# A conformer convolution beside a DeltaNet scan: when GpSimd joins in, where the channel sums stand, which PSUM banks the copies take

## The chip, the cores and the metric

The kernel runs on one core of one Trainium2 chip. A core has five engines that work side by side, each through a queue of its own in order: TensorE (PE, matmuls, with its weight loads shown apart as PEld), VectorE (DVE), ScalarE (ACT), GpSimd (POOL) and SyncE (SP, which here only starts transfers). The metric is the device time of one execution in microseconds, as a median of repeated executions.

## The reference, cut to what matters

One layer on 512 frames of 2048 channels, in float32. A shared projection `proj = h @ w_in` feeds two mixers. Branch A is a gated DeltaNet: 16 heads, a short convolution, a recurrence over chunks of 64 frames, and `y_a = o_a @ w_br_a`. Branch B is a convolution module. What the change touches:

```python
u = jax.nn.glu(glu_in, axis=-1)                 # 16 blocks of 128 channels x 512 frames
u = causal_depthwise_conv(u, w_dw[i]) + b_dw[i] # 31 taps
u = jax.nn.silu(layernorm(u, ln_g[i], ln_b[i])) * jax.nn.silu(z_b)
y_b = u @ w_br_b[i]
mixed = (gate_a * y_a + gate_b * y_b) @ w_out[i]
x = x + rmsnorm(mixed, g_post[i])
e = p[i] @ w_ple_proj[i]
x = x + rmsnorm(jax.nn.sigmoid(x @ w_ple_gate[i]) * e, g_ple[i])
```

The layer norm runs over the channels, so it needs the sum of all 16 convolved blocks.

## The kernel before, in words

**Products.** A float32 product is made of three matmuls on rounded halves: high by high, high by low, low by high (L184, L186, L188 for a block of `proj`; L1090, L1092, L1094 for the branches; L1548 to L1550 for the last product). Weights come in pieces of 128 x 512. For each, SP loads `raw`, ACT casts the high half (L127) and L128 subtracts to get the low half `w`; four pieces fit in the ring, and the program prepares each up to three pieces ahead of its use. `low_part[0]` names the engine that does L128: DVE at first, GpSimd from a certain place in the program, DVE again from the layer norm on. In the stage of branch A a piece serves 12 matmuls of 512 columns.

**Stages.** About 50 to 510 us: gate products. 530 to 1494: `q`, `k`, `v` blocks for the heads, with the recurrence of each group of heads (`group`, `head_scan`) woven in between. 1494 to 1845: the rest of the GLU blocks and branch A. 1846 to 1925: layer norm. To 2094: branch B. To 2260: `w_out` by a Strassen scheme, with the steps of the post norm (`post`) at its end, first for the lower 256 frames (LOW) and then for the upper (HIGH). To 2436: the last product, `gemm_tm`. The rest is the tail.

**Weaving.** Side work is written as generators. `tick()` follows each matmul; a generator moves on when as many matmuls have passed as it yielded. A scheduler then sets each engine's queue from the order of the program; `pin` keeps an instruction in the order in which it was written. Whatever stands in an engine's queue waits for what stands ahead of it.

**The convolution.** `evac_glu_b` (sigmoid on ACT) and `evac_glu_a` (product on DVE, L981) leave a block `sg` in SBUF. `convs` takes the blocks that wait, one after another: `near` starts `y` on ACT (L933) and 30 taps on DVE follow (L954), the accumulator `uc` in SBUF. The first channel begins while the recurrence still runs, with `sg` read from SBUF. Once the PSUM pool `ups` exists, `near` first copies the block to PSUM (L930, `up`), and the taps read `up`. `side_convs` does two of the 16 channels on ACT (products, L972) and GpSimd (sums, L973). `filtered` gathers the channel sum `acc` on GpSimd: a copy for the first channel (L918), an addition for the others (L920).

**At the end of the recurrence** stand, for each pair of heads, L733 (DVE), L735 (GpSimd), L739 (DVE, the normed output `O`), L744 (PE, transposes `po`) and L749 (DVE, out of `po`). After it the pools of the heads close: two PSUM banks of weight sums and four of the scan come free. Four of `yps` and two of `ups` are taken in their place. `split_oa` makes the halves of the heads' outputs (L1067 on ACT, L1069 on GpSimd).

**Later steps.** `branch` sums a block of y over 16 pieces into four banks and evacuates them (L1102). `layer_norm` sums over channels with a matmul by ones (`sum_ps`, L1143), and later spreads the reciprocal deviation with another (`rstd_ps`, L1170). `post` scales, adds x again (L1460), transposes (L1466) and splits (L1470).

Of the kernel before, what the change touches and what calls it, by code (L numbers as in the profile page):

```python
# [12 lines left out]
ALU = mybir.AluOpType  # L13
# [4 lines left out]
NTT = T // P  # L18
D = 2048
NK = D // P  # L20
# [7 lines left out]
CP = 10  # L28
# [53 lines left out]
def _body(ctx, tc, A, out):  # L82
    nc = tc.nc
    PSUM = bass.MemoryType.PSUM
# [209 lines left out]
    def stepper(gen, n=1):  # L294
        def f(k=None):
            for _ in range(n):
                next(gen, None)
        return f
# [605 lines left out]
    waiting = deque()  # L904
    taken = set()
    scanning = [-1]

    def evac_glu_b(i):
        def f(ps):
# [5 lines left out]
    def filtered(i, y):  # L915
        if not acc:
            acc.append(slots.tile([P, T], F32, tag="s", name="acc"))
            nc.gpsimd.tensor_copy(acc[0], y)  # L918
        else:
            nc.gpsimd.tensor_tensor(acc[0], acc[0], y, ALU.add)  # L920
        done.add(i)

    def near(held=True):
# [10 lines left out]
        return i, u, y  # L934

    def pace(s):
        return (3 + s % 2) if ups else CP

    def convs():
        ready = last = None  # L940
        while scanning[0] < NH // 2 - 1:
            yield 4
        while len(done) < NK:
            ready = ready or near()
            if not ready:
                if last and len(taken) == NK:
                    filtered(*last)
                    last = None
                yield 1
                continue  # L950
            (i, u, y), ready = ready, None
            w0 = V_DW + i * TAPS
            for s in range(1, TAPS):
                pin(nc.vector.scalar_tensor_tensor(y[:, s:], u[:, 0:T - s], vv(w0 + TAPS - 1 - s), y[:, s:], ALU.mult, ALU.add))  # L954
                if s == 28 and last:
                    filtered(*last)
                    last = None
                if s == 24:
                    ready = near()
                yield pace(s)  # L960
            nc.sync.dma_start(u_dram[i], y)
            last = i, y

    def side_convs():
        for _ in range(SIDE):
            while not waiting:
                yield 1
            i, u, y = near(False)
            w0 = V_DW + i * TAPS
            for s in range(1, TAPS):  # L970
                pr = s2.tile([P, T], F32, tag="s2", name="pr")
                nc.scalar.activation(pr[:, s:], u[:, 0:T - s], AF.Copy, scale=vv(w0 + TAPS - 1 - s))  # L972
                pin(nc.gpsimd.tensor_tensor(y[:, s:], y[:, s:], pr[:, s:], ALU.add))  # L973
                yield 18
            nc.sync.dma_start(u_dram[i], y)
            filtered(i, y)
# [75 lines left out]
    s2_ctx = ExitStack()  # L1052
    lop = s2_ctx.enter_context(tc.tile_pool(name="lop", bufs=LOP))
    s2 = s2_ctx.enter_context(tc.tile_pool(name="s2", bufs=40 - LOP))
    yps = s2_ctx.enter_context(tc.tile_pool(name="yps", bufs=4, space=PSUM))
    ups = s2_ctx.enter_context(tc.tile_pool(name="ups", bufs=2, space=PSUM))
    cpool[:] = [s2, "s2"]
    low_part[0] = nc.gpsimd

    def low(n, name, dt=F32R):  # L1060
        return lop.tile([P, T], dt, tag="lop", name=name) if n < LOP else s2.tile([P, T], dt, tag="s2", name=name)
# [14 lines left out]
    def branch(W, j, q, lhs, evac, side=None):  # L1076
        prep_src.extend([W[j, 2 * q], W[j, 2 * q + 1]])

        def job():
            if q == 0:  # L1080
                branch_ps[j] = [yps.tile([P, T], F32, tag="y", name="yp") for _ in range(NTT)]
            ps = branch_ps[j]
            for k in range(4 * q, 4 * q + 4):
                wh, wl = next_piece()
                if side:
                    side(k)
                for tt in range(NTT):
                    b = slice(tt * P, (tt + 1) * P)
                    lh, ll = lhs[k]
                    mm(ps[tt], lh[:, b], wh, start=k == 0, stop=False)  # L1090
                    tick()
                    mm(ps[tt], lh[:, b], wl, start=False, stop=False)  # L1092
                    tick()
                    mm(ps[tt], ll[:, b], wh, start=False, stop=k == NK - 1)  # L1094
                    tick()
            if q == 3:
                for tt in range(NTT):
                    evac(j, tt, ps[tt])
        jobs.append(job)

    def evac_ya(j, tt, ps):
# [32 lines left out]
    def layer_norm():  # L1134
        for i in range(NK):
            while i not in done:
                yield
            u_t[i] = hp("ur")
            nc.sync.dma_start(u_t[i], u_dram[i])
            yield 1  # L1140
        low_part[0] = nc.vector
        pm = ups.tile([P, T], F32, tag="u", name="sum_ps")
        mm(pm, ones, acc[0], start=True, stop=True)  # L1143
        mean = ups.tile([P, T], F32, tag="u", name="mean_ps")
        nc.scalar.activation(mean, pm, AF.Copy, scale=1.0 / D)
        acc2 = hp("acc2")
        yield 6
        for i in range(NK):
            u = u_t[i]
            pin(nc.vector.tensor_tensor(u, u, mean, ALU.subtract))  # L1150
            sq = hp("lsq") if i else acc2
            nc.scalar.activation(sq, u, AF.Square)
            if i:
                pin(nc.vector.tensor_tensor(acc2, acc2, sq, ALU.add))
            yield 7
        pvr = ups.tile([P, T], F32, tag="u", name="var_ps")
        for tt in range(NTT):
            mm(pvr[:, tt:tt + 1], acc2[:, tt * P:(tt + 1) * P], ones[:, 0:1], start=True, stop=True)
        var = lnp.tile([P, NTT], F32, name="var")
        nc.vector.tensor_scalar(var, pvr[:, 0:NTT], 1.0 / D, EPS, ALU.mult, ALU.add)  # L1160
        rst = lnp.tile([P, NTT], F32, name="rst")
        nc.gpsimd.tensor_tensor(rst, var, mhalf_c[:, 0:NTT], ALU.pow)
        dg = hp("dg")
        for tt in range(NTT):
            nc.vector.tensor_scalar(dg[:, tt * P:(tt + 1) * P], ident, rst[:, tt:tt + 1], None, ALU.mult)
        for i in range(3):
            load_zb(i)
        yield 12
        rstd = ups.tile([P, T], F32, tag="u", name="rstd_ps")
        mm(rstd, ones, dg, start=True, stop=True)  # L1170
        yield 6
        for i in range(NK):
            u = u_t[i]
            pin(nc.vector.tensor_tensor(u, u, rstd, ALU.mult))
            nc.scalar.activation(u, u, AF.Silu, scale=vv(V_LNG + i), bias=vv(V_LNB + i))
            yield 6
            if i + 3 < NK:
                load_zb(i + 3)
            nc.vector.tensor_tensor(u, u, zb[i], ALU.mult)
            uh = low(0, "uh")  # L1180
            nc.scalar.copy(uh, u)
            ul = low(LOP if i < 33 - LOP else 0, "ul")
            nc.vector.tensor_tensor(ul, u, uh.bitcast(F32), ALU.subtract)
            uT[i] = (uh, ul)
            yield 6
# [269 lines left out]

    def post(tts, xr):
        rm = inv_rms(ssm[:, tts[0]:tts[0] + 2, :], f"m{tts[0]}")
        for j in range(4):
            for n, tt in enumerate(tts):
                nc.vector.scalar_tensor_tensor(x1[tt][j], x1[tt][j], rm[:, n:n + 1], xr.pop((tt, j)), ALU.mult, ALU.add)  # L1460
            yield
            for k2 in (2 * j, 2 * j + 1):
                ps = bank()
                for n in range(4):
                    k = 2 * k2 + n // 2
                    nc.tensor.transpose(ps[:, n * P:(n + 1) * P], x1[tts[n % 2]][j][:, (k % 4) * P:(k % 4 + 1) * P], ident)  # L1466
                xh = unit(HP_, "xh", F32R)
                nc.scalar.copy(xh, ps)
                xl = unit(HP_, "xl", F32R)
                nc.vector.tensor_tensor(xl, ps, xh.bitcast(F32), ALU.subtract)  # L1470
                x1T[k2, tts[0] // 2] = (xh, xl)
                yield
# [67 lines left out]
    def gemm_tm(lhs, evac, tts=ALL, side=None):  # L1540
        ps = {tt: bank() for tt in tts}
        for k in range(NK):
            wh, wl = next_piece()
            if side:
                side(k)
            for tt in tts:
                lh, ll = lhs(k, tt)
                mm(ps[tt], lh, wh, start=k == 0, stop=False)  # L1548
                mm(ps[tt], lh, wl, start=False, stop=False)  # L1549
                mm(ps[tt], ll, wh, start=False, stop=k == NK - 1)  # L1550
        for tt in tts:
            evac(tt, ps[tt])
# [52 lines left out]
    gp = bcast_row(A["g_ple"], 0)  # L1605
    load_e(0)
    pgen = post(HIGH, xr)
    gemm_tm(x1_lhs, ple_evac(0, gp), LOW, stepper(pgen))
    for _ in pgen:
        pass  # L1610
    gemm_tm(x1_lhs, ple_evac(0, gp), HIGH)
# [87 lines left out]
```

## Time and profile before

| | |
|---|---|
| median of 3 runs | 2446.0 us (2445.83 to 2446.65) |
| the profiled execution | 2447.55 us, span 2445.8 us |
| mean granted TensorE clock | 0.998 |
| PE busy | 2414.0 us (99%) |
| DVE busy | 1792.4 us (73%) |
| ACT busy | 1208.8 us (49%) |
| POOL busy | 507.0 us (21%) |

Times in the views count from the start of the span. In a row of the timeline stand the start, the busy time, the engine, the line and operation, what is written from what, and in brackets the engine's idle time just before it and what ended that. A row of waits names the engine and its line, what released it, and then the total, the number and the longest. A row of windows has, for each engine, the busy time and in brackets the instructions, then the granted clock, the share of the transfers and GB/s.

### The profile page before, as it was taken

What the parts mean: (1) busy time and instruction counts of PE and PEld (TensorE: products, weight loads), DVE (VectorE), ACT (ScalarE), POOL (GpSimd) and SP (SyncE); (2) the same over time, 40 slices, a digit from 0 to 9 for tenths busy, and PEclk for the clock granted to TensorE, in tenths of its full rate; (3) what the DMA queues carried; (4) which work ended last, traced back from release to release, by engine and by line L of the source; (5) the groups of instructions that cost most, each with busy time, mean ns of one, the idle gap of its engine ahead of it and who ended that gap; (6) DMA issues with size and microseconds to landing.
All of it is one profiled execution on the core that took longest, in us unless ns stands there. A gap on an engine that the chain in (4) does not pass through costs nothing.

```text
span 2445.8 us, 33732 instructions
## 1 busy us (share of the span) xinstructions
PE 2414.0 (99%) x11962; PEld 1985.5 (81%) x11962; DVE 1792.4 (73%) x3345; ACT 1208.8 (49%) x2357; POOL 507.0 (21%) x531
## 2 busy tenths in 40 slices
PE   8999999999999999999999998999999999999998
PEld 7888888887888888888888887888887888787886
DVE  7877888777677676867777678998998654667644
ACT  6455544554655656455555544454324533554532
POOL 0001110013213021132300005998740000000000
PEclk9999999999999999999999999999999999999999
DMA  7577776666536263556622222443534333665552
GB/s 270 162 199 199 202 201 208 207 162 204 175 119 185 87 185 93 171 168 178 181 90 90 67 91 79 138 137 104 170 118 166 131 122 99 232 216 173 188 173 77
DMA packets 145289, 380.21 MB, mean 155 GB/s; under 512 B 16352, under 2 KB 24800, under 8 KB 145120
## 3 DMA queue, kind: packets, MB, share of 16 engines
q1 hardware_dynamic: 119008, 319.32, 39.4%
q0 software_dynamic: 23808, 54.54, 10.3%
q10 hardware_dynamic: 2304, 4.20, 0.5%
q8 instruction: 94, 1.54, 0.3%
q14 instruction: 75, 0.61, 0.1%
HBM read 329.75 MB, written 48.23 MB: 155 GB/s over the span
## 4 chain that ended last, share of the span: by engine, by line
PE 89%; DVE 3%; POOL 2%; DMA 2%; issue 2%; ACT 2%; SPq 0%; POOLq 0%; DVEq 0%; ACTq 0%
PE g L186 13%; PE g L188 13%; PE g L184 13%; PE zp L423 6%; PE zp L421 6%; PE zp L422 5%; PE yp L1090 4%; PE yp L1094 4%; PE yp L1092 4%; PE f L1382 2%; PE f L1383 2%; PE f L1384 2%; PE f L1548 2%; PE f L1549 2%; PE f L1550 2%
## 5 line engine op out<-in xcount | busy, mean ns | idle before, releaser
L188 PE MATMUL g<-hh,w 128*128 128x512 f32 x1536 | 610.6, 397 | 4.1 <-POOL w L128 4.1
L186 PE MATMUL g<-hl,w 128*128 128x512 f32 x1536 | 611.3, 398 | 0.0
L184 PE MATMUL g<-hh,w 128*128 128x512 f32 x1536 | 609.5, 397 | 0.0
L127 ACT CAST w<-raw 128x512 fp32r<-128x512 f32 x588 | 357.9, 618 | 446.8 <-PE g L188 172.8
L128 DVE TENSOR_TENSOR w<-raw,w 128x512 fp32r<-128x512 f32 x464 | 321.5, 700 | 169.2 <-ACT w L127 166.6
L188 PEld LDWEIGHTS g<-hh,w 128*128 128x128 f32 x1536 | 289.8, 189 | 61.5 <-POOL w L128 5.4
L186 PEld LDWEIGHTS g<-hl,w 128*128 128x128 f32 x1536 | 289.6, 189 | 55.8 <-issue 1.4
L184 PEld LDWEIGHTS g<-hh,w 128*128 128x128 f32 x1536 | 289.9, 189 | 54.7 <-ACT w L127 0.9
L954 DVE SCALAR_TENSOR_TENSOR uc<-up,vec,uc 128x506 f32<-128x506 f32 (+29 forms) x390 | 284.0, 734 | 11.9
L128 POOL TENSOR_TENSOR w<-raw,w 128x512 fp32r<-128x512 f32 x124 | 161.4, 1314 | 136.7 <-DVE uc L954 74.5
L656 DVE SCALAR_TENSOR_TENSOR cv<-g,vec,cv 128x511 f32<-128x511 f32 x144 | 106.4, 739 | 27.2 <-ACT cv L654 26.6
L1090 PE MATMUL yp<-w,uh 128*128 128x512 f32 x256 | 100.2, 392 | 0.7 <-DVE gt L1102 0.7
L1094 PE MATMUL yp<-w,ul 128*128 128x512 f32 x256 | 100.1, 392 | 0.0
L1090 PE MATMUL yp<-w,oh 128*128 128x512 f32 x256 | 100.0, 393 | 0.0
L1092 PE MATMUL yp<-w,uh 128*128 128x512 f32 x256 | 100.0, 391 | 0.0
L1092 PE MATMUL yp<-w,oh 128*128 128x512 f32 x256 | 99.6, 389 | 0.0
L1094 PE MATMUL yp<-w,ol 128*128 128x512 f32 x256 | 99.1, 389 | 0.0
L842 DVE TENSOR_TENSOR prod<-UT,VT 128x2 f32<-128x2 f32 (+30 forms) x248 | 88.4, 356 | 6.5
L1006 POOL DMA_DIRECT2D wsum<-in_w_out x96 | 76.1, 847 | 71.2 <-DMA wsum<-in_w_out 32.9
L1326 POOL TENSOR_TENSOR rmsm<-totm,mhalf_c 128x2 f32<-128x2 f32 x2 | 2.4, 1198 | 378.3 <-DVE totm L1324 378.3
L973 POOL TENSOR_TENSOR uc<-uc,pr 128x511 f32<-128x511 f32 (+29 forms) x60 | 77.8, 1297 | 3.7 <-ACT pr L972 2.5
L1382 PE MATMUL f<-wsp,oph 128*128 128x512 f32 x192 | 75.6, 394 | 1.7 <-ACT wsp L1363 1.7
(386 smaller groups left out, 4952.5 us busy)
## 6 DMA issues: line engine op xcount, KB each, us to landing
raw<-in_w_in SPq DMA_DIRECT2D x194, 512.0 KB, 3.4
wsum<-in_w_out POOLq DMA_DIRECT2D x96, 256.0 KB, 5.4
raw<-in_w_ple_gate SPq DMA_DIRECT2D x40, 512.0 KB, 3.5
wo_sums<-wsum POOLq DMA_DIRECT2D x64, 256.0 KB, 4.1
raw<-in_w_br_a SPq DMA_DIRECT2D x32, 512.0 KB, 3.4
raw<-in_w_br_b SPq DMA_DIRECT2D x32, 512.0 KB, 3.3
raw<-in_w_ga SPq DMA_DIRECT2D x24, 512.0 KB, 4.7
raw<-in_w_gb SPq DMA_DIRECT2D x24, 512.0 KB, 4.5
```

The source lines that it names most:

```text
L127: nc.scalar.copy(hi, rq)
L128: low_part[0].tensor_tensor(lo, rq, hi.bitcast(F32), ALU.subtract)
L184: mm(ps, wh, rh, start=(k == 0), stop=False)
L186: mm(ps, wh, rl, start=False, stop=False)
L188: mm(ps, wl, rh, start=False, stop=(k == NK - 1))
L421: mm(ps[pr][t], lh, wh, start=q + n == 0, stop=False)
L423: mm(ps[pr][t], lh, wl, start=False, stop=q == 3 and n == 1)
L954: pin(nc.vector.scalar_tensor_tensor(y[:, s:], u[:, 0:T - s], vv(w0 + TAPS - 1 - s), y[:, s:], ALU.mult, ALU.add))
L1090: mm(ps[tt], lh[:, b], wh, start=k == 0, stop=False)
L1092: mm(ps[tt], lh[:, b], wl, start=False, stop=False)
L1094: mm(ps[tt], ll[:, b], wh, start=False, stop=k == NK - 1)
L1382: mm(ps, lh, wh[:, c], start=kk == 0, stop=False)
```

## The change

Line numbers after the first edit are one higher, and up to eight higher at the end. The edits:

- `taken_ps`: the engine of L128 goes over to GpSimd only when `convs` has written the last tap of the channel that was under way when `ups` came to be; `side_convs` waits for the same mark, and until then that channel goes at a pace of four matmuls per tap, not three and four in turn.
- The two instructions of `filtered` are pinned.
- `ups` is made before `yps`, so that it takes the first banks that come free.
- `branch` evacuates each of the four banks as soon as its last matmul is written, not all four behind the last.
- In the layer norm, `yield 8` stands before the channel sum, and `yield 18` in place of `yield 12` before the spread.
- In `post`, the scaling and addition for step j + 1 stand before the transposes of step j; and in the last product over LOW, the steps for HIGH are not taken at pieces 1 to 3.

```diff
+    taken_ps = [False]
@@ filtered
-            nc.gpsimd.tensor_copy(acc[0], y)
+            pin(nc.gpsimd.tensor_copy(acc[0], y))
         else:
-            nc.gpsimd.tensor_tensor(acc[0], acc[0], y, ALU.add)
+            pin(nc.gpsimd.tensor_tensor(acc[0], acc[0], y, ALU.add))
@@ pace
-        return (3 + s % 2) if ups else CP
+        return (3 + s % 2 if taken_ps[0] else 4) if ups else CP
@@ convs
             nc.sync.dma_start(u_dram[i], y)
             last = i, y
+            if ups and not taken_ps[0]:
+                taken_ps[0] = True
+                low_part[0] = nc.gpsimd
@@ side_convs
-            while not waiting:
+            while not waiting or not taken_ps[0]:
                 yield 1
@@ after the heads
+    ups = s2_ctx.enter_context(tc.tile_pool(name="ups", bufs=2, space=PSUM))
     yps = s2_ctx.enter_context(tc.tile_pool(name="yps", bufs=4, space=PSUM))
-    ups = s2_ctx.enter_context(tc.tile_pool(name="ups", bufs=2, space=PSUM))
     cpool[:] = [s2, "s2"]
-    low_part[0] = nc.gpsimd
@@ branch
                     mm(ps[tt], ll[:, b], wh, start=False, stop=k == NK - 1)
                     tick()
-            if q == 3:
-                for tt in range(NTT):
-                    evac(j, tt, ps[tt])
+                    if k == NK - 1:
+                        evac(j, tt, ps[tt])
@@ layer_norm
         low_part[0] = nc.vector
+        yield 8
         pm = ups.tile([P, T], F32, tag="u", name="sum_ps")
...
-        yield 12
+        yield 18
         rstd = ups.tile([P, T], F32, tag="u", name="rstd_ps")
@@ post
-        for j in range(4):
+
+        def with_x(j):
             for n, tt in enumerate(tts):
                 nc.vector.scalar_tensor_tensor(x1[tt][j], x1[tt][j], rm[:, n:n + 1], xr.pop((tt, j)), ALU.mult, ALU.add)
-            yield
+        with_x(0)
+        yield
+        for j in range(4):
+            if j < 3:
+                with_x(j + 1)
             for k2 in (2 * j, 2 * j + 1):
@@ the last product
-    gemm_tm(x1_lhs, ple_evac(0, gp), LOW, stepper(pgen))
+    gemm_tm(x1_lhs, ple_evac(0, gp), LOW, lambda k: next(pgen, None) if k not in (1, 2, 3) else None)
```

**Where GpSimd's queue moves.** The engine is GpSimd, the place the beginning of branch A. `ors` is the norm step of the recurrence, `w` the low half of a piece, `uc` the side channel, `acc` the channel sum. Before:

```order
L735 TENSOR_TENSOR ors_14057<-ors,mhalf_c 128x4
L128 TENSOR_TENSOR w<-raw,w 128x512
L973 TENSOR_TENSOR uc<-uc,pr 128x511
L973 TENSOR_TENSOR uc<-uc,pr 128x510
L128 TENSOR_TENSOR w<-raw,w 128x512 x2
L973 TENSOR_TENSOR uc<-uc,pr 128x509
L973 TENSOR_TENSOR uc<-uc,pr 128x508
L128 TENSOR_TENSOR w<-raw,w 128x512 x2
L973 TENSOR_TENSOR uc<-uc,pr 128x507
L128 TENSOR_TENSOR w<-raw,w 128x512
L918 COPY acc<-uc 128x512
L128 TENSOR_TENSOR w<-raw,w 128x512
```

Now, from just below the first two low parts on:

```order
L977 TENSOR_TENSOR uc<-uc,pr 128x511
L977 TENSOR_TENSOR uc<-uc,pr 128x510
L128 TENSOR_TENSOR w<-raw,w 128x512 x2
L977 TENSOR_TENSOR uc<-uc,pr 128x509
L1072 TENSOR_TENSOR ol<-oa,oh 128x512
L128 TENSOR_TENSOR w<-raw,w 128x512 x2
L977 TENSOR_TENSOR uc<-uc,pr 128x508
L977 TENSOR_TENSOR uc<-uc,pr 128x507
L128 TENSOR_TENSOR w<-raw,w 128x512 x2
L1072 TENSOR_TENSOR ol<-oa,oh 128x512
L977 TENSOR_TENSOR uc<-uc,pr 128x506
L919 COPY acc<-uc 128x512
```

Ten low parts have gone to DVE; the first on GpSimd is that of the eleventh piece. The copy `acc<-uc`, which stood just ahead of the low part of the twelfth piece, now stands behind eight low parts (two above the excerpt), six side taps and two `ol`.

**Where DVE and ACT move.** The end of the recurrence on DVE, before:

```order
L733 SCALAR_TENSOR_TENSOR ors<-ms,epsq 128x4
L739 SCALAR_TENSOR_TENSOR O<-O,ors_14053,za 128x128 x4
L749 TENSOR_SCALAR oa<-po,vec 128x4x64 x2
L733 SCALAR_TENSOR_TENSOR ors<-ms,epsq 128x4
L739 SCALAR_TENSOR_TENSOR O<-O,ors_14057,za 128x128 x4
L749 TENSOR_SCALAR oa<-po,vec 128x4x64 x2
L954 SCALAR_TENSOR_TENSOR uc<-sg,vec,uc 128x502
```

Now, in two pieces, the end of the recurrence and the end of the first channel 21 rows below it:

```order
L955 SCALAR_TENSOR_TENSOR uc<-sg,vec,uc 128x500
L733 SCALAR_TENSOR_TENSOR ors<-ms,epsq 128x4
L128 TENSOR_TENSOR w<-raw,w 128x512
L739 SCALAR_TENSOR_TENSOR O<-O,ors_14053,za 128x128 x4
L733 SCALAR_TENSOR_TENSOR ors<-ms,epsq 128x4
L955 SCALAR_TENSOR_TENSOR uc<-sg,vec,uc 128x499
L739 SCALAR_TENSOR_TENSOR O<-O,ors_14057,za 128x128 x4
L749 TENSOR_SCALAR oa<-po,vec 128x4x64 x2
L955 SCALAR_TENSOR_TENSOR uc<-sg,vec,uc 128x498
```

```order
L955 SCALAR_TENSOR_TENSOR uc<-sg,vec,uc 128x483
L955 SCALAR_TENSOR_TENSOR uc<-sg,vec,uc 128x482
L985 TENSOR_TENSOR sg<-g,sg 128x512
L749 TENSOR_SCALAR oa<-po,vec 128x4x64 x2
L955 SCALAR_TENSOR_TENSOR uc<-up,vec,uc 128x511
```

The second pair of L749 has gone from ahead of the last 21 taps of the first channel to behind them, five low parts and a GLU product. On ACT the copies `up` stood within the last norm step of the recurrence (L730); now they stand behind it, after five casts, and the start of both channels, two products for the side channel and the next casts follow them:

```order
L931 COPY up<-sg 128x512 x2
L934 ACTIVATE uc<-up,vec 128x512
L934 ACTIVATE uc<-sg,vec 128x512
L976 ACTIVATE pr<-sg,vec 128x511
L976 ACTIVATE pr<-sg,vec 128x510
L127 CAST w<-raw 128x512 x2
L976 ACTIVATE pr<-sg,vec 128x509
```

The banks that `up` takes are now the two of the `po` transposes, which the second pair of L749 reads last; before, they were banks of the scan.

**Where PE's queue moves.** The engine is PE, the place the last product over LOW, into which the transposes of HIGH are woven (`f<-cst,snap`). Before, the first of them follow the 15th matmul of that product:

```order
L1548 MATMUL f<-w,xh 128x512
L1549 MATMUL f<-w,xh 128x512
L1550 MATMUL f<-w,xl 128x512
L1466 MATMUL f<-cst,snap 128x128 x2
L1548 MATMUL f<-w,xh 128x512
L1549 MATMUL f<-w,xh 128x512
L1466 MATMUL f<-cst,snap 128x128 x6
```

Now they follow the 24th, four at a time:

```order
L1556 MATMUL f<-w,xh 128x512
L1557 MATMUL f<-w,xh 128x512
L1558 MATMUL f<-w,xl 128x512
L1474 MATMUL f<-cst,snap 128x128 x4
L1556 MATMUL f<-w,xh 128x512
```

Nine matmuls stand in front of the first transposes that stood behind them.

## The prediction, written before the changed kernel was run

> **What bounds the kernel now.** First the page's busy times and the list of PE's waits:
>
> ```profile
> PE 2414.0 (99%) x11962; PEld 1985.5 (81%) x11962; DVE 1792.4 (73%) x3345; ACT 1208.8 (49%) x2357; POOL 507.0 (21%) x531
> ```
>
> ```profile
> PE g L188 <- POOL w L128: 4.1, 2, 3.5
> PE po L744 <- DVE O L739: 3.1, 4, 1.0
> PE f L1382 <- ACT wsp L1363: 1.7, 1, 1.7
> PE f L1382 <- DVE gb L1200: 0.8, 1, 0.8
> PE rstd_ps L1170 <- DVE dg L1165: 0.8, 1, 0.8
> ...
> PE f L1466 <- DVE snap L1460: 0.7, 1, 0.7
> PE yp L1090 <- DVE gt L1102: 0.7, 1, 0.7
> ...
> PE sum_ps L1143 <- POOL acc L920: 0.6, 1, 0.6
> PE f L1466 <- DVE c L1460: 0.6, 1, 0.6
> ```
>
> TensorE is busy for 99% of the span, and the change takes no matmul away: all it can win is a share of these waits and of what follows them. The first has a tail that the list leaves out. PE's timeline there, then windows of it and of a quiet stretch (PE first, the granted clock third from the end):
>
> ```profile
> 1517.45 0.39 PE L186 MATMUL g<-hl,w 128*128 128x512 f32 x1
> 1521.29 0.79 PE L188 MATMUL g<-hh,w 128*128 128x512 f32 x1 [3.45 <-POOL w L128]
> ...
> 1526.96 0.40 PE L184 MATMUL g<-hh,w 128*128 128x512 f32 x1
> ```
>
> ```profile
> 1520.00:1525.00 5.00, 3.71 (x9) 2.94 (x10) 4.82 (x8) 0.00 (x0) 5.00 (x6) 0.51 0.78 259
> 1535.00:1585.00 50.00, 50.00 (x222) 41.40 (x221) 47.67 (x69) 23.68 (x41) 49.39 (x41) 1.00 0.44 138
> ```
>
> At a clock of 1.00, 222 matmuls take 50 us, 0.225 us each (0.227 in single rows). Between 1517.45 and 1526.96 lie 15 such steps, 3.4 us at that pace; they took 9.51. So the place costs 6.1 us: 3.6 of standing, and 2.5 because the clock is at 0.51 for a while behind it.
>
> The Trainium skill, "TensorE: Matmul & The Clock Gate", Part 1, has the array fall to half clock after an idle window of about 3.4 us and come back after a busy window as long. By that the slow stretch would cost about 1.7 us (an estimate from the page) and the place 5.3; the rows have 6.1, and the measurement decides.
>
> Who is late stands in GpSimd's timeline:
>
> ```profile
> 1510.25 1.72 POOL L128 TENSOR_TENSOR w<-raw,w 128x512 fp32r<-128x512 f32 x1
> 1519.40 0.61 POOL L918 COPY acc<-uc 128x512 f32<-128x512 f32 x1 [7.43 <-DVE uc L954]
> 1519.97 1.27 POOL L128 TENSOR_TENSOR w<-raw,w 128x512 fp32r<-128x512 f32 x1
> ```
>
> GpSimd is free and stands idle for 7.43 us ahead of the sum's copy, which waits for the last DVE tap of the first channel; the low part that PE lacks is queued behind it. Why that tap is late shows in DVE's groups over three stretches, 1455 to 1468, 1497.4 to 1511.9 and 1512 to 1519.2:
>
> ```profile
> L954 DVE SCALAR_TENSOR_TENSOR uc<-sg,vec,uc 128x510 f32<-128x510 f32 (+3 forms) x4 | 2.9, 735 | 0.0
> ```
>
> ```profile
> L954 DVE SCALAR_TENSOR_TENSOR uc<-sg,vec,uc 128x499 f32<-128x499 f32 (+8 forms) x9 | 14.8, 1646 | 0.3
> ```
>
> ```profile
> L954 DVE SCALAR_TENSOR_TENSOR uc<-sg,vec,uc 128x491 f32<-128x491 f32 (+9 forms) x10 | 8.2, 817 | 0.4
> ```
>
> The same tap, both tensors in SBUF, takes 735 ns without GpSimd, 1646 while GpSimd works without a pause, and 817 once it stands idle (one of those ten still overlaps).
>
> **The late low part: gain 6.1.** In the new order the copy of `acc` stands behind eight low parts and six side taps, so this wait can't recur in that form. Its place is taken by a longer chain, which holds the thirteenth piece: first channel on DVE, second pair of L749, copies `up`, ACT's queue, GpSimd's queue. DVE's timeline, then the groups of the stage, the last two from 1540 on:
>
> ```profile
> 1490.76 2.19 DVE L739 SCALAR_TENSOR_TENSOR O<-O,ors,za 128x128 f32<-128x128 f32 x4 [1.13 <-POOL ors L735]
> 1493.38 0.88 DVE L749 TENSOR_SCALAR oa<-po,vec 128x256 f32<-128x256 f32 x2 [0.42 <-PE po L744]
> ...
> 1519.26 0.74 DVE L954 SCALAR_TENSOR_TENSOR uc<-up,vec,uc 128x511 f32<-128x511 f32 x1
> 1519.92 0.68 DVE L981 TENSOR_TENSOR sg<-g,sg 128x512 f32<-128x512 f32 x1
> ```
>
> ```profile
> L127 ACT CAST w<-raw 128x512 fp32r<-128x512 f32 x126 | 77.0, 617 | 134.9 <-PE yp L1094 61.6 <-PE g L188 49.7 <-POOL w L128 19.1
> L972 ACT ACTIVATE pr<-sg,vec 128x511 f32<-128x511 f32 (+29 forms) x60 | 40.9, 707 | 36.9 <-POOL uc L973 35.9 <-POOL acc L920 0.8
> L933 ACT ACTIVATE uc<-up,vec 128x512 f32<-128x512 f32 x13 | 10.1, 775 | 4.2 <-POOL uc L973 2.5 <-DMA u_dram<-uc 1.5
> L930 ACT COPY up<-sg 128x512 f32<-128x512 f32 x11 | 6.4, 585 | 3.8 <-DVE uc L954 3.8
> L128 DVE TENSOR_TENSOR w<-raw,w 128x512 fp32r<-128x512 f32 x8 | 5.5, 685 | 1.5 <-ACT w L127 1.5
> ```
>
> ```profile
> L128 POOL TENSOR_TENSOR w<-raw,w 128x512 fp32r<-128x512 f32 x105 | 135.1, 1298 | 53.4 <-ACT w L127 51.6 <-issue 1.4
> L973 POOL TENSOR_TENSOR uc<-uc,pr 128x501 f32<-128x501 f32 (+29 forms) x50 | 63.0, 1260 | 0.9
> ```
>
> The second group of L739 ended at 1490.76 + 2.19 = 1493.0, and I take the same moment for the new order. Behind it DVE then has the first pair of L749 (0.88), 17 taps of the first channel, five low parts, a GLU product and the second pair. From tap to the next instruction it is 0.66 us (1519.26 to 1519.92, a duration of 0.74 less an overlap of 0.08); with that overlap off each, the sum is 0.8 + 17 x 0.66 + 5 x 0.61 + 0.6 + 0.8 = 16.5, ending at 1509.5. GpSimd starts its first low part, of the eleventh piece, when that is cast; before, this was at 1510.25. One or two taps may meet it, at 0.9 more each (1646 less 735). I take 1511 for the moment T at which DVE is through, 1509.5 to 1513 as bounds.
>
> From T on ACT: two copies, two channel starts and two products, 2 x 0.585 + 2 x 0.775 + 2 x 0.707, less six overlaps of 0.08: 3.7, with the second product as the last; the cast of the thirteenth piece ends 0.5 later. GpSimd begins its first tap at about T + 3.1, ends the second at T + 5.6 (2 x 1.26), and the low part at T + 6.9, so at 1517.9. PE wanted the twelfth piece 0.23 behind 1517.45 and wants the thirteenth 12 matmuls later, at 1520.4, or 1519.9 with the half microsecond that it gains ahead (below). The margin is 2.0 us; the wait begins for T over 1513.0, which is the upper bound. So I take the whole 6.1 and price the late case among the rivals.
>
> What this moves elsewhere: ten low parts are 10 x 0.685 = 6.9 us more on DVE, in a stretch where it was slowed by more than that; DVE waits some 2.5 us for the first `up` tap, and nobody waits for that tap. The side channels begin some 15 us later: 60 taps, one per 18 matmuls of 0.227, are 245 us, over at about 1760, while the channel sum is wanted at 1845. The pins and the pace of 4 cost nothing under the same cover; without it, a tap late at the end would delay the channel sum one for one.
>
> **The end of the recurrence: gain 0.5.** PE waits for 3.1 us there. In the new order the first pair of L749 no longer stands between the two norm groups on DVE: 0.88, and the 0.5 or so that it waits for PE (0.42 in the second pair's row), less a tap of 0.66 that now stands ahead of the first L733; the low part and the other tap fall into the waits for GpSimd (1.13). That leaves about 0.7. PE still has 18 matmuls of `proj` to put between its last scan step and the last transposes. Three low parts between the scan's steps may cost up to 0.6 each, where they stand ahead of a state update: minus 0.5 to 1.5 in all, and I take 0.5.
>
> **The small waits: gain 1.4.** For the evacuation and for HIGH, PE's timeline:
>
> ```profile
> 1913.14 0.39 PE L1094 MATMUL yp<-w,ol 128*128 128x512 f32 x1
> 1914.18 0.47 PE L1090 MATMUL yp<-w,uh 128*128 128x512 f32 x1 [0.66 <-DVE gt L1102]
> ```
>
> ```profile
> 2260.54 0.39 PE L1550 MATMUL f<-w,xl 128*128 128x512 f32 x1
> 2261.63 0.44 PE L1466 MATMUL f<-cst,snap 128*128 128x128 f32 x2 [0.71 <-DVE snap L1460]
> ```
>
> - Evacuation: 1914.18 less 1913.14 less 0.23 is 0.81 lost. Banks are now read while others are still summed, but DVE's normal work of the layer norm stands between; half of it, 0.35 (0 to 0.8).
> - HIGH: nine matmuls more ahead of the transposes are 2.0 us, more than the whole 1.09 between the two rows: the wait goes, 0.75. LOW has nothing more ahead of its first transposes, and its 0.6 stays.
> - `yield 8` and `yield 18`: the channel sum moves 5 matmuls (1.1 us) in PE's queue, but DVE's last tap stands behind one low part and one tap more (0.685 + 0.735): 0.6 stays. Between the variance and the spread there are 6 matmuls as before: 0.8 stays. Bounds 0 to 1.4 together.
> - The second wait for GpSimd's low part is 4.1 less 3.5, 0.6, at 1680, where GpSimd's order is shifted: it goes or stays, 0.3.
>
> The sum: 6.1 + 0.5 + 0.35 + 0.75 + 0.3 = 8.0. Against the profiled execution, 2447.55 (span 2445.8), that is 2439.5; against the median of the runs, 2446.0, which lies 1.5 lower, 2438.0. The runs of the new kernel are medians too, so 2438.
>
> **The rivals.**
>
> *The new chain is late by little.* DVE ends the first channel at 1514 to 1516 instead of 1511, from contention with three to five more instructions at 0.9 or from low parts that wait on their casts. PE then stands for 1 to 3 us at the thirteenth piece. For it speaks the thin margin; against it, that only two low parts can run on GpSimd before T. A gain of 5 to 7: about 2440.
>
> *GpSimd is full, and the stall only moves.* The window 1535 to 1585 has it busy for 49.39 of 50. The new kernel starts its side channels later, into the same load; each time that a low part falls behind a side tap by more than the ring's slack, PE waits 0.6 (as at 1680) up to 1.3 (a tap). Four such are 2.4 to 5 us: 2441 to 2443. Against it: for these 50 us PE did not wait at all.
>
> *All the small waits go.* The channel sum 0.6, the spread 0.8, the rest of the evacuation 0.45, the norm of LOW 0.6: 2.4 more, 2435.5. It needs the orders to give more slack than the rows read there.
>
> *The slower side: the taps are slow for a reason other than GpSimd.* If a tap from SBUF takes 1646 ns here whoever runs beside it, 17 of them are 17 x 0.91 = 15.5 later: T = 1525, the thirteenth piece 12 us late, with 2.5 for the clock 14.5 lost against 8 won: 2452.5. It turns slower when T passes 1518.5 (5.5 of standing + 2.5), beyond what can be told from no change when T passes 1523.5. Against it: 735 before and 817 after GpSimd's work, on the same tensors.
>
> *The change does less than it says*: only the GpSimd part acts, 6.1, and the end of the recurrence gives back 1: 2441.
>
> **How the numbers follow.** My forecast has 0.55, the late chain 0.15, the full GpSimd 0.10, all small waits 0.10, the slower side 0.04, less than it says 0.06. A measurement of this kernel can tell about 0.2%, 4.9 us, from no change, so faster means below 2441.1. Forecast and small waits lie there, of the late chain two thirds, of the full GpSimd and of the last a third each: 0.80. Slower than 2450.9 is the slower side at its full price and a rest for what I did not see: 0.04. Within lies 0.16. The range: the bounds of the forecast's terms (the end of the recurrence 1 either way, small waits 1.4 either way) give 2436 to 2440.5; with the small waits gone below and the full GpSimd above, 2434.5 to 2443.
>
> **What will show it.** Right, if PE's wait for GpSimd's low part around 1517 is gone and the clock stands at 1.00 in all windows from 1500 to 1535; if the taps from `sg` there take about 735 ns; if the first `up` tap starts near 1514; if PE has no wait for HIGH's `snap`. Wrong, if a wait for a low part of 1 us or more stands between 1515 and 1525, if several stand up to 1700, or if the waits at the end of the recurrence grow.

## The result, and the profile after

The changed kernel takes 2437.3 us (median of 6, 2436.45 to 2439.83) against 2446.32 us of the kernel before in the same comparison: a ratio of 0.9966, with a 95% interval of 0.9956 to 0.9977. The forecast was 2438.0, with 2434.5 to 2443.0 as the range. The profiled execution took 2438.2 us, 9.35 less than the one before.

The same views, after. Busy times and PE's waits, without those of the first 500 us, which the change does not touch:

```profile
PE 2409.8 (99%) x11962; PEld 1983.6 (81%) x11962; DVE 1785.5 (73%) x3355; ACT 1208.0 (50%) x2357; POOL 491.8 (20%) x521
```

```profile
PE f L1385 <- ACT wsp L1366: 1.7, 1, 1.7
PE po L744 <- DVE O L739: 1.5, 2, 0.8
...
PE yp L1093 <- DVE gt L1104: 0.9, 1, 0.9
PE f L1385 <- DVE gb L1203: 0.9, 1, 0.9
PE rstd_ps L1173 <- DVE dg L1168: 0.7, 1, 0.7
...
PE sum_ps L1146 <- POOL acc L921: 0.4, 1, 0.4
```

No wait for a low part from GpSimd is left, and none for HIGH's `snap`. The windows where PE stood before have a clock of 1.00:

```profile
1515.00:1520.00 5.00, 5.00 (x23) 3.90 (x22) 4.79 (x7) 4.48 (x9) 4.92 (x5) 1.00 0.00 0
1520.00:1525.00 5.00, 5.00 (x24) 4.14 (x23) 4.75 (x8) 5.00 (x9) 5.00 (x5) 1.00 0.31 105
```

The chain that was to take the old one's place, in the timelines of DVE, ACT, GpSimd and PE:

```profile
1503.25 6.52 DVE L955 SCALAR_TENSOR_TENSOR uc<-sg,vec,uc 128x487 f32<-128x487 f32 x6
1509.69 0.68 DVE L985 TENSOR_TENSOR sg<-g,sg 128x512 f32<-128x512 f32 x1
1510.29 0.86 DVE L749 TENSOR_SCALAR oa<-po,vec 128x256 f32<-128x256 f32 x2
1513.04 11.64 DVE L955 SCALAR_TENSOR_TENSOR uc<-up,vec,uc 128x511 f32<-128x511 f32 x15 [1.89 <-ACT uc L934]
```

```profile
1511.18 1.11 ACT L931 COPY up<-sg 128x512 f32<-128x512 f32 x2 [3.30 <-DVE oa L749]
...
1514.84 1.13 ACT L127 CAST w<-raw 128x512 fp32r<-128x512 f32 x2
```

```profile
1514.46 2.69 POOL L977 TENSOR_TENSOR uc<-uc,pr 128x511 f32<-128x511 f32 x2 [5.20 <-ACT pr L976]
1517.10 2.56 POOL L128 TENSOR_TENSOR w<-raw,w 128x512 fp32r<-128x512 f32 x2
```

```profile
1518.17 0.39 PE L186 MATMUL g<-hl,w 128*128 128x512 f32 x1
1518.46 0.50 PE L188 MATMUL g<-hh,w 128*128 128x512 f32 x1
```

DVE is through at 1510.29 + 0.86 = 1511.15; the copies `up`, held for 3.30 us by the pair of L749, start at once. The thirteenth piece's low part is the first of the two from 1517.10, ready near 1518.4; PE starts its matmul 0.29 behind the one before, not 0.23. It came just in time: 0.06 us is lost here, and 0.11 at the next matmul.

**A ledger that the start doesn't blur.** The stretch up to the last scan steps ended between 1453.8 and 1455.9 us in the executions here, though the kernels' work there is the same. So I take, for each kernel, the time from one row of the last scan steps to PE's last matmul. Before, then after:

```profile
1455.54 0.61 PE L703 MATMUL psA<-S,kq 128*128 128x128 f32 x4
...
2436.04 0.40 PE L1627 MATMUL f<-hih,xl 128*128 128x512 f32 x1
```

```profile
1455.64 0.61 PE L703 MATMUL psA<-S,kq 128*128 128x128 f32 x4
...
2426.66 0.40 PE L1635 MATMUL f<-hih,xl 128*128 128x512 f32 x1
```

980.5 and 971.0: the late stretch is 9.5 us shorter. From start to start of PE's matmuls, with the usual step (0.227 for 512 columns) taken off each, this is where they came from:

| place | before, lost | after, lost | gain | forecast |
|---|---|---|---|---|
| low part at 1517, with the slow clock | 6.3 | 0.2 | 6.1 | 6.1 |
| low parts at 1627 and 1680 | 1.5 | 0 | 1.5 | 0.3 |
| end of the recurrence (transposes `po`) | 4.3 | 2.4 | 1.9 | 0.5 |
| channel sum | 0.8 | 0.6 | 0.2 | 0 |
| spread (`rstd_ps`) | 0.9 | 0.9 | 0 | 0 |
| evacuation, and the gaps behind it to 1920 | 0.9 | 2.1 | -1.2 | 0.35 |
| HIGH's transposes | 0.9 | 0 | 0.9 | 0.75 |
| sum | | | 9.4 | 8.0 |

### The profile page after: what moved, and what is told of

It is laid out like the page before. It is cut to its first block, busy times and chain, and to the rows that moved or that the text cites. A ratio compares the mean times of both kernels' runs of the same rounds, so it can differ in the third digit from the quotient of the medians.

```text
span 2436.4 us, 33721 instructions
## 1 busy us (share of the span) xinstructions
PE 2409.8 (99%) x11962; PEld 1983.6 (81%) x11962; DVE 1785.5 (73%) x3355; ACT 1208.0 (50%) x2357; POOL 491.8 (20%) x521
## 4 chain that ended last, share of the span: by engine, by line
PE 94%; DVE 3%; ACT 1%; issue 1%; DMA 1%; POOL 0%; SPq 0%; DVEq 0%; POOLq 0%; ACTq 0%
PE g L186 14%; PE g L188 14%; PE g L184 14%; PE zp L422 6%; PE zp L421 6%; PE zp L423 6%; PE yp L1095 4%; PE yp L1097 4%; PE yp L1093 4%; PE f L1385 2%; PE f L1386 2%; PE f L1387 2%; PE f L1558 2%; PE f L1557 2%; PE f L1556 2%; PE psB L709 1%
## 5 line engine op out<-in xcount | busy, mean ns | idle before, releaser
L128 DVE TENSOR_TENSOR w<-raw,w 128x512 fp32r<-128x512 f32 x474 | 327.2, 697 | 180.3 <-ACT w L127 177.4
L955 DVE SCALAR_TENSOR_TENSOR uc<-up,vec,uc 128x497 f32<-128x497 f32 (+29 forms) x390 | 282.3, 734 | 13.2 <-ACT uc L934 1.9
L128 POOL TENSOR_TENSOR w<-raw,w 128x512 fp32r<-128x512 f32 x114 | 146.6, 1301 | 59.6 <-ACT w L127 57.8
```

Of the source, the lines that this page charges most:

```text
L128: low_part[0].tensor_tensor(lo, rq, hi.bitcast(F32), ALU.subtract)
```

## The experiments

The question behind them: which of the edits carries the gain, and is the cause of the stall the place of the channel sum's copy in GpSimd's queue, or the two engines slowing each other? In the results "late stretch" is the time between the two rows above, one profiled execution each; it repeated within 0.15 us where a kernel was run twice. Times are medians, with the ratio to the kernel before and its interval.

### The sums pinned, and nothing else

```diff
-            nc.gpsimd.tensor_copy(acc[0], y)
+            pin(nc.gpsimd.tensor_copy(acc[0], y))
...
-            nc.gpsimd.tensor_tensor(acc[0], acc[0], y, ALU.add)
+            pin(nc.gpsimd.tensor_tensor(acc[0], acc[0], y, ALU.add))
```

> The kernel before with the two instructions of the channel sum pinned, nothing else. GpSimd's queue then has the copy of acc behind five low parts and four side taps more; GpSimd goes on working beside the first channel's taps. Theory (the contention is the root): the wait at the twelfth piece goes, but the last ten taps from sg stay at 1646 ns instead of 817, so the first channel ends near 1528 instead of 1519; the GLU product L981 stands behind it on DVE and holds the bank that PE wants at about 1520, so PE waits there for DVE for some 8 us and 2.5 more at half clock: 2446 to 2452. Rival (the place of the copy in the queue is the whole cause): the 6.1 us are won, about 2440.

Measured: 2452.35 us (2449.73 to 2453.95), ratio 1.0022 (1.0013 to 1.0031); late stretch 985.7, 5.2 longer. PE's largest wait, the groups of DVE from 1496 to 1527, its timeline, and a window of PE alone:

```profile
PE g L184 <- DVE sg L981: 8.7, 1, 8.7
```

```profile
L954 DVE SCALAR_TENSOR_TENSOR uc<-sg,vec,uc 128x500 f32<-128x500 f32 (+18 forms) x19 | 31.1, 1634 | 0.7
```

```profile
1506.67 19.89 DVE L954 SCALAR_TENSOR_TENSOR uc<-sg,vec,uc 128x493 f32<-128x493 f32 x12
1526.48 0.74 DVE L954 SCALAR_TENSOR_TENSOR uc<-up,vec,uc 128x511 f32<-128x511 f32 x1
1527.14 0.67 DVE L981 TENSOR_TENSOR sg<-g,sg 128x512 f32<-128x512 f32 x1
```

```profile
1525.00:1530.00 5.00, 2.04 (x5) 0.50 0.50 157
```

The time lies just above the expected range. The copy no longer holds GpSimd, GpSimd goes on, and so 19 taps take 1634 ns each. The first channel ends at 1526.5 (expected: near 1528), and PE waits 8.7 us (expected: some 8) for the GLU product queued behind it. Removing the queue's stop made the kernel slower: the idle 7.43 us of GpSimd before had been what let DVE finish. The rival, that the place of the copy is the whole cause, falls.

### GpSimd's part alone

```diff
+    taken_ps = [False]
-        return (3 + s % 2) if ups else CP
+        return (3 + s % 2 if taken_ps[0] else 4) if ups else CP
...
+            if ups and not taken_ps[0]:
+                taken_ps[0] = True
+                low_part[0] = nc.gpsimd
...
-            while not waiting:
+            while not waiting or not taken_ps[0]:
...
-    low_part[0] = nc.gpsimd
```

> The kernel before with GpSimd's part beginning behind the first channel (the engine of the low parts, the side channels' wait, the pace), without pins, without the order of the banks, without the later edits. The copy of acc stands behind only four low parts' worth of queue: two low parts, two side taps. Theory: the first channel ends near 1510, before GpSimd reaches that copy, so the stall of 6.1 and the waits for low parts at 1627 and 1680 go, while the end of the recurrence and HIGH stay: 2438.5 to 2440.5. Rival (the pins are needed): a wait of 2 us or more for a low part stays near 1517.

Measured: 2437.19 us (2434.84 to 2438.16), ratio 0.9958 (0.9944 to 0.9973); late stretch 970.7, 9.8 shorter. That is below the expected range. No wait for a low part is left, without a pin. The first channel ends at 1511.8 (expected 1510), so GpSimd still stops at the copy of `acc`, but only for 1.81 us and at no cost to PE:

```profile
1511.97 0.61 POOL L919 COPY acc<-uc 128x512 f32<-128x512 f32 x1 [1.81 <-DVE uc L955]
1512.54 2.55 POOL L128 TENSOR_TENSOR w<-raw,w 128x512 fp32r<-128x512 f32 x2
```

This edit by itself gives the whole gain of the change. It also shortens the end of the recurrence (PE's waits for `po` are 1.4 here, 3.1 before), which I had put down to the order of the banks. HIGH's 0.9 is still lost here, and goes in each kernel with the edit of `post` and of the last product; what all the other edits give and take adds up to about nothing.

### Either half of GpSimd's part

Only the side channels wait (the first), or only the low parts stay on DVE (the second):

```diff
+            if ups:
+                taken_ps[0] = True
...
-            while not waiting:
+            while not waiting or not taken_ps[0]:
```

> The kernel before, where only the two side channels wait for the end of the first channel; the low parts go over to GpSimd where they did. GpSimd then has one low part per 2.72 us beside the taps from sg, instead of being full. Theory (each GpSimd instruction beside such taps costs DVE about 0.96 us: 14.8 us for nine taps less 9 x 0.735, over 8 to 9 instructions of GpSimd): 21 taps are 13.9 plus 0.35 of their own length, the first channel ends near 1515.7, the copy of acc is free in time, and the stall shrinks from 6.1 to 0 to 0.5: about 2440. Rival (it is the low parts, not GpSimd's load, that slow the taps): the first channel ends at 1518 or later and PE still stands for 2 us or more: 2443 or more.

```diff
+            if ups and not taken_ps[0]:
+                taken_ps[0] = True
+                low_part[0] = nc.gpsimd
...
-    low_part[0] = nc.gpsimd
```

> The kernel before, where only the low parts stay on DVE until the first channel is done; the side channels begin where they did. GpSimd has one side tap per 4.08 us there. Theory: four or five side taps cost DVE 4 to 5 us, the first channel ends near 1513 to 1514, no low part stands behind the copy of acc before that; the stall goes, and the waits at 1627 and 1680 go or shrink: 2437 to 2440. Rival (both parts are needed): a wait of 1 us or more for a low part or for DVE's sg between 1515 and 1530.

Measured: 2440.61 us (2439.59 to 2442.19), ratio 0.9975 (0.9966 to 0.9984), late stretch 974.1; and 2440.68 us (2439.13 to 2442.38), ratio 0.9977 (0.9968 to 0.9986), late stretch 974.3. Each half wins about 6 of the 9.8. With the side channels later, in the timelines of DVE, GpSimd and PE:

```profile
1492.17 21.70 DVE L955 SCALAR_TENSOR_TENSOR uc<-sg,vec,uc 128x502 f32<-128x502 f32 x21
```

```profile
1513.93 0.61 POOL L919 COPY acc<-uc 128x512 f32<-128x512 f32 x1 [6.67 <-DVE uc L955]
```

```profile
1519.68 0.50 PE L188 MATMUL g<-hh,w 128*128 128x512 f32 x1 [0.82 <-POOL w L128]
```

The 21 taps take 21.7 us, 1.03 each. At 0.66 each they would take 13.9, so they lose 7.8, with 7 instructions of GpSimd beside them. In the pinned kernel the same 21 taps take 33.24 us and lose 19.4, beside 20 instructions of GpSimd. About 1 us is lost per instruction of GpSimd either way. The first channel ends at 1513.8 (expected 1515.7), the copy of `acc` still stands in the queue and stops GpSimd for 6.67, and PE loses some 2 us for low parts near 1516, 1520 and 1526 (expected 0 to 0.5). Another 1.5 us goes at the end of the recurrence: after two waits of 0.99 and 0.87 us for L739, which stand in the kernel before too, PE's clock is at 0.50 from 1487.3 to 1489.6, where the kernel before has 1.00. With the low parts on DVE, the groups of DVE from 1494 to 1510:

```profile
L955 DVE SCALAR_TENSOR_TENSOR uc<-sg,vec,uc 128x496 f32<-128x496 f32 (+8 forms) x9 | 11.4, 1263 | 0.2
L128 DVE TENSOR_TENSOR w<-raw,w 128x512 fp32r<-128x512 f32 x4 | 6.0, 1496 | 0.0
```

DVE's low parts, which also read two tensors from SBUF, take 1496 ns beside the side taps instead of 685. I had not priced that. The first channel ends at 1515.6 (expected 1513 to 1514), and the copy of `acc` again stops GpSimd, for 6.28 us, with a low part behind it. PE lost 1.3 near 1510 for a low part of DVE's, 1.3 near 1525 for one of GpSimd's and 0.8 near 1673. The time is a little above the expected range. The rival holds: both halves are needed for the whole.

### The banks as before

```diff
-    ups = s2_ctx.enter_context(tc.tile_pool(name="ups", bufs=2, space=PSUM))
     yps = s2_ctx.enter_context(tc.tile_pool(name="yps", bufs=4, space=PSUM))
+    ups = s2_ctx.enter_context(tc.tile_pool(name="ups", bufs=2, space=PSUM))
```

This is the changed kernel with the one edit undone.

> The changed kernel with yps made before ups, as it was. The copies up then stand within the last norm step again and wait for nothing late. Theory: the thirteenth piece's low part has 3 us or more to spare (no gap in PE near 1518), and the end of the recurrence gives back its 1.5 to 1.9, since a pair of L749 stands between the two norm groups on DVE again: 2438 to 2439.5. Rival (the order of the banks pays nothing): 2437 or less.

Measured: 2435.14 us (2434.55 to 2435.97), ratio 0.9952 (0.9937 to 0.9967); late stretch 969.5, 1.5 shorter than the changed kernel's. The expectation fell: the end of the recurrence lost nothing (PE's waits for `po` are 1.4), nothing was lost near 1518, and the rival, that the order of the banks pays nothing, holds. The two were run side by side once more:

> The changed kernel itself, once more beside the next one on one chip. Theory (the order of the banks costs about 1.5 us of what the rest wins: 0.4 at the thirteenth piece and 1 in the layer norm's waits): 2437 to 2437.5, 1 to 2 above the next. Rival (the 2.2 us between their medians was chance): within 0.7 of it.

> The changed kernel with yps made before ups, again. Theory: 2435 to 2436, 1 to 2 below the changed kernel beside it. Rival: within 0.7 of it.

2437.31 us (2436.56 to 2437.66), ratio 0.9965 (0.9953 to 0.9978), and 2436.34 us (2434.95 to 2437.36), ratio 0.9960 (0.9948 to 0.9973). They lie 0.97 apart, between the theory (1 to 2) and the rival (0.7), and the intervals overlap, so the times don't settle it. The late stretches do for these executions: 970.98 and 969.68, after 971.02 and 969.54. The order of the banks costs 1.3 to 1.5 us as it stands. About 0.4 of that lies between the last scan steps and branch A, the rest in the layer norm and branch B. The converse, the order of the banks on the kernel before with nothing else, wasn't run.

### The evacuations and the longer yields

The changed kernel with the evacuations behind the loop:

```diff
-                    if k == NK - 1:
-                        evac(j, tt, ps[tt])
+            if q == 3:
+                for tt in range(NTT):
+                    evac(j, tt, ps[tt])
```

> The changed kernel with the four evacuations behind the loop, as before. Theory: the wait of PE for gt in the layer norm (0.92 in one piece, 1.07 from start to start, after 0.81 before) falls to about 0.8, and with it the time by 0.3 to 0.5: 2436.5 to 2437. Rival (evacuating in the loop pays elsewhere in branch A): 2437.5 or more.

Measured: 2438.5 us (2436.62 to 2441.48), ratio 0.9966 (0.9953 to 0.9979); late stretch 972.6, 1.6 longer. The theory fell, the rival holds. PE now waits twice for an evacuation, at 1857 and at 1908; the first of them:

```profile
1857.78 0.47 PE L1093 MATMUL yp<-w,oh 128*128 128x512 f32 x1 [1.33 <-DVE gt L1105]
```

Without the longer yields as well:

```diff
-        yield 8
...
-        yield 18
+        yield 12
```

> The changed kernel with the evacuations behind the loop and without the two longer yields. With the evacuations alone undone, PE waited 1.33 and 1.24 for gt. Theory (yields and evacuations act together: the yields push the evacuations behind more of DVE's layer norm, and evacuating in the loop gives that back): the two waits fall to 0.7 each or less, 2436 to 2437.5. Rival (the evacuations alone decide): both waits stay at 1.2 or more, 2438 to 2439.

Measured: 2435.56 us (2434.79 to 2435.63), ratio 0.9959 (0.9943 to 0.9974); late stretch 969.4, 1.6 shorter than the changed kernel's. That is below the expected range. PE has no wait for `gt` in branch A at all. And with the banks as before and the evacuations in the loop, the yields alone undone:

> The changed kernel with yps made before ups and without the two longer yields of the layer norm. Theory (the yields move the two matmuls among others and shift no wait by more than 0.5): within 1 us of the kernel with yps first, 2434.5 to 2436. Rival (the yields pay what they are written for): the waits for acc and for dg grow by 1 us or more together.

Measured: 2435.45 us (2434.76 to 2436.53), ratio 0.9955 (0.9938 to 0.9971); late stretch 969.1, the shortest of all. The waits for `acc` and `dg` stay at 0.5 each: the yields don't pay. Start to start, PE's losses at these places of the layer norm are:

| kernel | channel sum | evacuation and the wait near 1856 | spread |
|---|---|---|---|
| before | 0.8 | 0.8 | 0.9 |
| changed | 0.6 | 1.3 | 0.9 |
| evacuations behind the loop | 1.2 | 2.9 | 0.7 |
| evacuations behind, no longer yields | 1.2 | 0 | 0.9 |
| banks as before | 0.6 | 0.8 | 0.7 |

So the two edits act together in the kernels with the new order of the banks: with the longer yields the evacuations come late, and evacuating in the loop repairs half of that. With neither, nothing is lost there. This does not carry over to the old order of the banks. The kernel with GpSimd's part alone has neither edit and loses 0.8 near 1857, and the one with the banks as before has both and loses 0.8 near 1856; the profile puts both waits down to ACT (L1155), not to an evacuation. Evacuating in the loop does pay at the channel sum, 0.6 lost against 1.2. Which instruction the yields push ahead of the evacuations in each case I have not traced further.

## Why the prediction was right, step by step

- **What bounds it**, right. PE's clock and its busy share are what the change could win on, and the gain is the sum of waits.
- **The late low part, 6.1**, right in size: 6.3 lost before, 0.2 after. I counted 15 steps between 1517.45 and 1526.96 where there are 14, so the place had cost 6.3. The cause, that DVE's taps and GpSimd slow each other, is shown: the pinned kernel, which only lets GpSimd go on, has its taps at 1634 ns and is slower, and each half of the load taken away gives the taps back a share.
- **The chain that replaces it.** DVE was to be through at 1511 and was at 1511.15. The margin of 2.0 us was wrong: none was left, 0.2 was lost. That the term came out nearly whole is luck. PE was earlier than I had it, since the end of the recurrence gained 1.9 and not 0.5, and GpSimd's low part was ready at 1518.4 and not 1517.9. The rival of the chain that is late by little had only a few tenths to go.
- **GpSimd is full**, the rival that stalls only move, did not come: from 1520 to 1760 it is busy for 219 us, 214 before, and PE never waits there. The wait at 1680, which I had half gone for 0.3, and a smaller loss at 1627 are gone for 1.5. Here the term was sized from the wait of 0.6 alone; start to start, with the slower matmuls around it, the place at 1680 cost 1.2.
- **The end of the recurrence, 0.5**: 1.9, and not by the mechanism given, the first pair of L749 no longer between the two norm groups. With GpSimd's part alone that pair still stands between them, and PE loses 2.2 at the transposes `po`, against 4.3 before and 2.4 in the changed kernel. In DVE's timeline there:

```profile
1486.94 1.14 DVE L739 SCALAR_TENSOR_TENSOR O<-O,ors,za 128x128 f32<-128x128 f32 x4 [0.90 <-POOL ors L735]
...
1488.67 0.48 DVE L749 TENSOR_SCALAR oa<-po,vec 128x256 f32<-128x256 f32 x1
...
1489.14 0.48 DVE L749 TENSOR_SCALAR oa<-po,vec 128x256 f32<-128x256 f32 x1
1490.41 1.14 DVE L739 SCALAR_TENSOR_TENSOR O<-O,ors,za 128x128 f32<-128x128 f32 x4 [0.79 <-POOL ors L735]
```

What changed is L739 itself: four took 2.16 and 2.19 us before, and take 1.14 now. Its eight executions between 1480 and 1494, before and in the changed kernel (shortest, median and longest in ns), and what GpSimd and PE did before:

```profile
L739 DVE SCALAR_TENSOR_TENSOR O<-O,ors,za x8: 337/350/1401, 1486.0 to 1492.6; 128x128 f32<-128x128 f32 x8
```

```profile
L739 DVE SCALAR_TENSOR_TENSOR O<-O,ors,za x8: 346/346/352, 1487.7 to 1491.2; 128x128 f32<-128x128 f32 x8
```

```profile
1486.48 1.29 POOL L128 TENSOR_TENSOR w<-raw,w 128x512 fp32r<-128x512 f32 x1 [0.49 <-ACT w L127]
...
1491.28 1.27 POOL L128 TENSOR_TENSOR w<-raw,w 128x512 fp32r<-128x512 f32 x1 [0.55 <-ACT w L127]
```

```profile
1487.98 0.33 PE L744 MATMUL po<-cst,O 128*128 128x128 f32 x1 [0.87 <-DVE O L739]
```

L739 reads two tensors from SBUF as the taps do. In each group of four, one ran beside a low part of GpSimd and took 1.4 us in place of 0.35, and PE waited for it. With the low parts on DVE none does. Where only the side channels wait, GpSimd keeps its low parts: one L739 still takes 1.36 us, and from the last scan steps to 1497 PE loses 5.4 us, 5.9 before and 3.8 in the changed kernel. So this gain, too, comes from the two engines slowing each other, and not from the order of L749 or of the banks; the prediction had not seen it.
- **HIGH, 0.75**: right, 0.9. **The channel sum and the spread, 0**: right, 0.2 and 0.
- **The evacuation, 0.35**: wrong in sign, -1.2. DVE's timeline after shows the step that failed, "half of it":

```profile
1902.54 0.68 DVE L1104 TENSOR_TENSOR gt<-yp,gt 128x512 f32<-128x512 f32 x1
1903.14 1.28 DVE L1186 TENSOR_TENSOR ul<-ur,uh 128x512 fp32r<-128x512 f32 x2
1904.34 1.27 DVE L1177 TENSOR_TENSOR ur<-ur,rstd_ps 128x512 f32<-128x512 f32 x2
1905.54 0.68 DVE L1104 TENSOR_TENSOR gt<-yp,gt 128x512 f32<-128x512 f32 x1
```

```profile
1904.97 0.39 PE L1093 MATMUL yp<-w,uh 128*128 128x512 f32 x1
1906.27 0.50 PE L1093 MATMUL yp<-w,uh 128*128 128x512 f32 x1 [0.92 <-DVE gt L1104]
```

Four norm instructions, 2.4 us, stand between two evacuations that stood side by side before. I had seen the order and judged that half the wait would stay. The longer yields, which I had costed at nothing, have a part in it, but not alone: the same yields with the banks as before leave no wait of PE for `gt`. How the edits bring it about together stays open.

- **The slower side**, taps slow for a reason other than GpSimd, is ruled out: in the changed kernel the six taps from 1503.25 take 6.52 us, 1.09 each, with two low parts of GpSimd beside them; the three from 1500.48, with GpSimd idle, take 2.25 us, 0.75 each; and in the pinned one a tap takes 1634 ns with GpSimd always at work. The sign "about 735 ns" thus came true only where GpSimd was idle.

The terms missed by 1.4 and 1.2 upward and by 1.5 downward, and the sum was off by 1.0 between the medians (9.0 for 8.0), by 1.4 in the table. That is luck as well as judgement.

## What to carry to other kernels

Where an engine stands idle in front of a wait, ask what its idleness lets another engine do, before taking the wait away. Work on a second engine is not always hidden: here each low part or side tap on GpSimd cost DVE's taps from SBUF about 1 us, and taps with an operand in PSUM nothing. Put it beside the latter, or behind the former. The same cost can sit at a place that looks like a question of order, as at the end of the recurrence. And of several edits made together, one may carry it all; small waits of half a microsecond come and go with the order that the scheduler finds, and each has to be seen in the trace of the whole.

## What the runs showed of the hardware

DVE and GpSimd slow each other when a DVE instruction reads two tensors from SBUF and a GpSimd instruction reads from SBUF too. In the pinned kernel a tap with two SBUF tensors takes 1634 ns and comes every 1.66 us (12 in 19.89), against 735 alone. The same holds for DVE's low parts (1496 against 685 on average, with only the low parts later), for L739 (1.4 us against 0.35, before), and for GpSimd's instructions (1.7 us beside an unbroken row of such taps, 1.27 without). The taps that read `up` from PSUM, and only `uc` from SBUF, show nothing of it. In the changed kernel from 1520 to 1760, where GpSimd is busy for 219 of 240 us:

```profile
L955 DVE SCALAR_TENSOR_TENSOR uc<-up,vec,uc 128x503 f32<-128x503 f32 (+5 forms) x296 | 216.5, 734 | 9.8
...
L977 POOL TENSOR_TENSOR uc<-uc,pr 128x509 f32<-128x509 f32 (+29 forms) x58 | 73.4, 1265 | 3.0 <-ACT pr L976 2.5
```

The Trainium skill, "SBUF — State Buffer", section "Who interferes with whom", states this: a VectorE instruction with two SBUF inputs contends with a GpSimd instruction that reads SBUF, one with a single SBUF input does not (outside its two-port modes), and the loser is blocked for the whole instruction. The traces agree on who contends. On the price they differ: one after the other in full would be 0.66 + 1.27 = 1.93 us per pair, and the runs show 1.66.
